# Who makes the lower halves of the first mixer's weights: VectorE instead of GpSimd, with two passes moved to ScalarE

## The chip, the cores and the metric

One core of a Trainium2 chip runs the whole program in one launch. The metric is the device time of one execution in microseconds (us), and the runs shown are compared by their median. A profile of one further execution is read beside them; its times count from the first instruction of the program.

## What is computed

The reference is a two-layer backbone for 256 latent tokens of width 1024, with 256 context tokens as a prefix. Layer 0 mixes tokens with a gated linear recurrence that runs in both directions (RG-LRU), layer 1 with a spatial-gating MLP, and each mixer is followed by a mixture of 64 experts with 8 chosen per token. The change concerns layer 0's mixer alone:

```python
def rglru_mixer(hx, hc, w_in, conv_w, conv_b, r_w, r_b, i_w, i_b, lam, w_out, ctx_out):
    gate_x, ux = jnp.split(hx @ w_in, 2, axis=-1)
    ux = dwconv_centred(ux, conv_w, conv_b)                    # 4 taps along the tokens
    uc = dwconv_centred(hc @ w_in[:, RNN_WIDTH:], conv_w, conv_b)
    for d in range(2):                                         # both directions
        a_c, b_c = lru_coeffs(flip(uc), r_w[d], r_b[d], i_w[d], i_b[d], lam[d], True)
        h_c = linear_scan(a_c, b_c)
        a_x, b_x = lru_coeffs(flip(ux), r_w[d], r_b[d], i_w[d], i_b[d], lam[d], False)
        b_x = b_x.at[:, 0].add(a_x[:, 0] * h_c[:, -1])
        yx = yx + flip(linear_scan(a_x, b_x))
    return (jax.nn.gelu(gate_x) * yx) @ w_out
```

`lru_coeffs` computes, from two 256x256 matrices per head (five heads), r = sigmoid(u r_w + r_b), i = sigmoid(u i_w + i_b), a = exp(8 r logsigmoid(lam)) and b = sqrt(1 - a^2) i u.

## The kernel before

Tokens lie along the free dimension and features along the 128 partitions, 256 latent and 256 context tokens side by side (512 columns). A float32 product is made of three fast ones (`mm3`, L309): both factors are split in an upper part that the fast format holds and a lower part (the rest), and high x high, high x low and low x high are summed, in this order.

**The weight stream.** Every weight tile is 128x2048 (1 MB) and comes in the order of one list, through a ring of eight buffers. For the mixers a tile is cut in four chunks of 128x512. The function `splitter` (L553) makes the two parts of each chunk: ScalarE copies the chunk to `wh` (L563), the engine that `eng(i, c)` names subtracts `wh` from the chunk and writes `wl` (L564). There are four buffers of each. A call `wq(q)` issues all splits up to chunk q+2, at that place of the program.

**The order.** The schedule is written out by hand (`manual_schedule`): each engine runs its instructions in the order in which the Python code issues them. For each head h the order is A(h), C(h), B(h) (L341), with pieces of another matrix product (`ada_step`, the fillers "F") between them; after the five heads come O(0) to O(3) and Q, the product with `w_out`.

- A(h) (L744): 48 matmuls of 512 columns, for two feature tiles i. When the last one of a tile is issued, `wq(q + 3 + 2 * i)` (L769) issues the splits of C's chunks 0, 1 (i=0) or 2, 3 (i=1). Then `conv` (L749): ScalarE applies one tap and the bias (L753), VectorE three taps (L755), a copy to the upper part `us` (L758) and the lower part (L759). At the end `release()` twice (L771) issues `B_end` for the two halves of head h-1.
- C(h) (L852): 48 matmuls of 256 columns and a gelu. Its `wq` calls, and those of the fillers behind it, issue the splits of B's four chunks.
- B(h) (L804): for two halves jt, 24 matmuls of 512 columns into four PSUM banks, that ScalarE takes out with tanh (L817); then a tanh and an exp for each direction (L822, L823), and VectorE's four passes over 128x1024 (L825 to L828). In the second half the calls at L816 and `wq(q + 5)` (L819) issue the splits of the next tile's four chunks, so they stand between the passes of the two halves.
- `B_end` (L831): ScalarE's square root over 128x1024 (L833, it needs another activation table), then on VectorE two memsets, a product (L836), four scans (L840, L843) and a sum (L845). `gated(h)` (L865), issued at the start of the next B, multiplies with the gelu (L868) and splits the product in `zh` and `zl` (L869, L870; on GpSimd for h < 4).
- After A(0) stands `decay()` (L786), a chain of 27 small VectorE instructions that needs a ScalarE exp first.

In the kernel before, `split_eng` (L704) names GpSimd for every tile but the last one (Q), that is for 19 tiles or 76 chunks.

Of the kernel before, what the change touches and what calls it, by code (L numbers as in the profile page):

```python
# [14 lines left out]
AF = mybir.ActivationFunctionType  # L15
OP = mybir.AluOpType
# [285 lines left out]
def _body(nc, tc, a, pp, rp, ps, ps1, dr):  # L302
    V, S, G, PE = nc.vector, nc.scalar, nc.gpsimd, nc.tensor
# [5 lines left out]
    def mm3(out, wh, wl, xh, xl, start, stop):  # L309

        mm(out, wh, xh, start, False)
        mm(out, wh, xl, False, False)
        mm(out, wl, xh, False, stop)

    def bank(shape=(P, 512)):
        return ps.tile(list(shape), F32, name="b")
# [22 lines left out]
    plan0, nf = [], 0  # L339
# [9 lines left out]
    for kind, i in plan0[1:]:  # L349
# [10 lines left out]
        elif kind == "F":  # L360
            l, c, k = fillers[i]
# [68 lines left out]
    onesf = pp.tile([P, P], F32, name="onesf")  # L430
# [23 lines left out]
    def warm(func):  # L454

        S.activation(out=warm_t, in_=onesf[:, 0:1], func=func)
# [96 lines left out]
    def splitter(tmp, tiles, eng, bufs=4):  # L553

        out = []

        def get(q, last=None):
            while len(out) < min(q + 3, last or 4 * len(tiles)):
                i, c = divmod(len(out), 4)
                t = st.tile(tiles[i])[:, 512 * c:512 * c + 512]  # L560
                hi = tmp.tile([P, 512], F32R, name="wh", bufs=bufs)
                lo = tmp.tile([P, 512], F32R, name="wl", bufs=bufs)
                S.copy(out=hi, in_=t)  # L563
                eng(i, c).tensor_tensor(out=lo, in0=t, in1=hi.bitcast(F32), op=OP.subtract)  # L564
                out.append((hi, lo))
                if c == 3:
                    st.free(tiles[i])
            return out[max(q, 0)]

        return get  # L570

    def cut(parts, c):
        return [x[:, c * P:c * P + P] for x in parts]
# [63 lines left out]
    def mixer0(rx):  # L637
      with tc.tile_pool(name="m0", bufs=1) as mp, tc.tile_pool(name="m0t", bufs=2) as tp:
# [3 lines left out]
        def h0(x, k):  # L642
            return h0t[2 * x + k // 4][:, k % 4, :]
# [57 lines left out]
        sx = mp.tile([P, 8], F32, name="sx")  # L701
        sc = mp.tile([P, 8], F32, name="sc")

        def split_eng(i, c):  # L704
            kind, j = plan0[users[i]]
            return G if kind in "ACOB" else V

        users = [i for i, e in enumerate(plan0) if e[0] != "F"]

        base = 8  # L710
        wq = splitter(tp, [2] + [base + i for i in users[1:]], split_eng)

        def first_quarter(b):

# [29 lines left out]
        def A(h, q):  # L744
            uc = tp.tile([P, 2, 2, T], F32, name="uc", bufs=2)
            us = tp.tile([P, 2, 2, 512], F32R, name="us", bufs=1)
            ucs[h] = uc, us

            def conv(i, p):  # L749
                ft = 2 * h + i  # L750
                pv = p.rearrange("p (s t) -> p s t", s=2)
                o = uc[:, i]
                S.activation(out=o, in_=pv, func=AF.Identity, scale=cw[:, 2, ft:ft + 1], bias=cb[:, ft:ft + 1])  # L753
                for kk, (d0, d1, s0_, s1_) in ((0, (2, T, 0, T - 2)), (1, (1, T, 0, T - 1)), (3, (0, T - 1, 1, T))):
                    V.scalar_tensor_tensor(out=o[:, :, d0:d1], in0=pv[:, :, s0_:s1_], scalar=cw[:, kk, ft:ft + 1],  # L755
                                           in1=o[:, :, d0:d1], op0=OP.mult, op1=OP.add)
                of = o.rearrange("p s t -> p (s t)")
                V.tensor_copy(out=us[:, 0, i, :], in_=of)  # L758
                V.tensor_tensor(out=us[:, 1, i, :], in0=of, in1=us[:, 0, i, :].bitcast(F32), op=OP.subtract)  # L759

            ps_ = [bank(), bank()]
            steps = [(i, k) for k in range(8) for i in range(2)] if h == 0 else [(i, k) for i in range(2) for k in range(8)]
            for i, k in steps:
                if h == 0 and i == 0 and k:
                    yield
                wc = divmod(2 * k + i if h == 0 else 8 * i + k, 4)
                mm3(ps_[i], *cut(wq(q + wc[0], 4 if h == 0 and k < 7 else None), wc[1]), h0(0, k), h0(1, k), k == 0, k == 7)
                if k == 7:
                    wq(q + 3 + 2 * i)  # L769
                    conv(i, ps_[i])  # L770
            release()  # L771
            release()
# [31 lines left out]
        def B(h, q):  # L804
            warm(AF.Exp)
            uc, us = ucs.pop(h)
            y = ys[h] = tp.tile([P, 2, T], F32, name="hf", bufs=4)

            for jt in range(2):
                ft = 2 * h + jt  # L810
                ta, te, ti = (tp.tile([P, 2, 512], F32, name=n, bufs=2) for n in ("T", "Tt", "I"))
                for g in range(2):
                    for d in range(2):
                        p = bank()
                        for k in range(2):
                            mm3(p, *cut(wq(q + 2 * jt + g), 2 * d + k), us[:, 0, k, :], us[:, 1, k, :], k == 0, k == 1)  # L816
                        S.activation(out=(ta, ti)[g][:, d, :], in_=p, func=AF.Tanh, scale=0.5, bias=(rb_, ib_)[g][:, d, ft:ft + 1])  # L817
                if jt:
                    wq(q + 5)  # L819
                for d in range(2):  # L820
                    n1, n2 = nz[:, d, ft:ft + 1], nz2[:, d, ft:ft + 1]
                    S.activation(out=te[:, d, :], in_=ta[:, d, :], func=AF.Tanh, scale=n1, bias=n1)  # L822
                    S.activation(out=ta[:, d, :], in_=ta[:, d, :], func=AF.Exp, scale=n2, bias=n2)  # L823
                uv = uc[:, jt].rearrange("p s t -> p (s t)").unsqueeze(1).to_broadcast([P, 2, 512])
                V.scalar_tensor_tensor(out=te, in0=ta, scalar=1.0, in1=te, op0=OP.add, op1=OP.mult)  # L825
                V.tensor_scalar(out=ta, in0=te, scalar1=-1.0, scalar2=1.0, op0=OP.mult, op1=OP.add)
                V.scalar_tensor_tensor(out=te, in0=te, scalar=2.0, in1=te, op0=OP.subtract, op1=OP.mult)
                V.scalar_tensor_tensor(out=ti, in0=ti, scalar=1.0, in1=uv, op0=OP.add, op1=OP.mult)  # L828
                held.append((h, jt, y, ta, te, ti))

        def B_end(h, jt, y, ta, te, ti):  # L831
# [29 lines left out]
        def release():  # L861
            if held:
                B_end(*held.popleft())
# [31 lines left out]
        for i, (kind, j) in enumerate(plan0):  # L895
            if kind == "F":
                l, c, k = fillers[j]
                ada_step(l, c, k, tp)
                wq(4 * sum(u < i for u in users) + 1)
                continue  # L900
            if kind == "O" and j == 0:
                tail = Tail(tp, 0, mod[:, 0, 2, :], rw, "hf", 4)
            if kind == "O" and j == 2:
                warm(AF.Sqrt)
            if kind == "B":
                while done:
                    gated(done.pop())
            if i == 0:
                deque(a0, 0)
                decay()  # L910
                continue
            n = st.reserve({"A": "a_in", "C": "a_in", "B": "gate", "O": "a_out", "Q": "a_out"}[kind])
            deque({"A": A, "B": B, "C": Cg, "O": O, "Q": Q}[kind](j, 4 * users.index(n - base)) or (), 0)
            if kind == "C":
                if j == 1:
                    late_small()
                    S.dma_start(rw, a["r_w"][:, 0])
                if j == 3:
                    V.tensor_copy(out=identb, in_=ident)
                    V.tensor_copy(out=ltrib, in_=C["ltri"])  # L920

                    V.tensor_scalar(out=later["rb"], in0=later["rb"], scalar1=0.5, scalar2=None, op0=OP.add)
                if j == 4:
                    st.grow(rx, "wx", 4)
# [676 lines left out]
    with tc.tile_pool(name="rx", bufs=1) as rx:  # L1601
        tail = mixer0(rx)
        tail = moe(0, tail)
        tail = mixer1(tail)
        moe(1, tail)
# [16 lines left out]
```

## Time and profile before

| | us |
|---|---|
| median of 3 runs | 1510.4 |
| lowest and highest | 1503.66, 1511.35 |
| the profiled execution's own time | 1504.02 |
| its span, first to last instruction | 1502.2 |

Busy shares of the span: TensorE (PE) 94%, VectorE (DVE) 51%, ScalarE (ACT) 35%, GpSimd (POOL) 29%. The mean granted TensorE clock is 0.973 of the full 2.4 GHz. In the rows below, a tile name stands with an arrow from what it is made of (`wl<-wr,wh`); "x" is a count; a bracket at the end of a timeline row is the engine's idle time before the instruction and what ended it. `PEld` is TensorE's weight load, which runs beside the matmuls. The first mixer runs from the start to about 262 us; the rest of the program does not contain any changed line.

### The profile page before, as it was taken

What the parts mean: (1) busy time and instruction counts of PE and PEld (TensorE: products, weight loads), DVE (VectorE), ACT (ScalarE), POOL (GpSimd) and SP (SyncE); (2) the same over time, 40 slices, a digit from 0 to 9 for tenths busy, and PEclk for the clock granted to TensorE, in tenths of its full rate; (3) what the DMA queues carried; (4) which work ended last, traced back from release to release, by engine and by line L of the source; (5) the groups of instructions that cost most, each with busy time, mean ns of one, the idle gap of its engine ahead of it and who ended that gap; (6) DMA issues with size and microseconds to landing.
All of it is one profiled execution on the core that took longest, in us unless ns stands there. A gap on an engine that the chain in (4) does not pass through costs nothing.

```text
span 1502.2 us, 27457 instructions
## 1 busy us (share of the span) xinstructions
PE 1410.3 (94%) x10752; PEld 983.3 (65%) x10752; DVE 766.5 (51%) x1388; ACT 518.9 (35%) x901; POOL 433.7 (29%) x454
## 2 busy tenths in 40 slices
PE   5999898789999999999999999789999999999998
PEld 4767677546567565565747899666656666566665
DVE  6899997623343434334346686532425333333434
ACT  4767673321222222222225544422212212212232
POOL 1666665412222113221101361322212212211210
PEclk9999999899999999999999999899999999999998
DMA  9776575589998999999999854469998999999994
GB/s 376 280 278 228 224 308 224 231 318 377 381 418 358 421 420 406 421 394 420 420 418 380 320 169 153 140 231 391 362 396 358 421 421 409 406 402 422 420 420 168
DMA packets 77446, 514.88 MB, mean 343 GB/s; under 512 B 9856, under 2 KB 10240, under 8 KB 17024
## 3 DMA queue, kind: packets, MB, share of 16 engines
q1 hardware_dynamic: 74720, 508.91, 83.8%
q10 hardware_dynamic: 2592, 4.16, 0.8%
q8 instruction: 86, 1.41, 0.4%
q14 instruction: 48, 0.39, 0.1%
HBM read 511.99 MB, written 1.05 MB: 342 GB/s over the span
## 4 chain that ended last, share of the span: by engine, by line
PE 59%; issue 13%; POOL 3%; DVE 2%; DMA 2%; ACT 1%; ACTq 0%; POOLq 0%; SPq 0%; DVEq 0%
PE b L307 49%; PE s L307 10%; DMA wr<-in_m_gu 2%; POOL S L1399 1%; POOL wl L564 1%; PE b L1475 1%; DMA wr<-in_m_dn 1%; DVE wl L564 1%; DVE h L948 0%; ACT wh L563 0%; PE b L1587 0%; DVE v L1004 0%; DVE xT L1115 0%; DVE v L1067 0%; DVE u L956 0%
## 5 line engine op out<-in xcount | busy, mean ns | idle before, releaser
L564 POOL TENSOR_TENSOR wl<-wr,wh 128x512 fp32r<-128x512 f32 x134 | 208.2, 1570 | 537.0 <-ACT wh L563 534.8
L307 PE MATMUL b<-wr,xg 128*32 128x512 f32 (+2 forms) x1496 | 301.1, 602 | 8.2 <-DMA wr<-in_m_gu 6.3
L563 ACT CAST wh<-wr 128x512 fp32r<-128x512 f32 x256 | 152.4, 618 | 200.8 <-PE b L307 93.6
L307 PE MATMUL b<-wx,xg 128*32 128x512 f32 (+1 forms) x712 | 196.1, 599 | 0.0
L307 PEld LDWEIGHTS b<-wr,xg 128*32 128x32 f32 (+2 forms) x1496 | 83.3, 119 | 130.6 <-issue 107.2
L307 PE MATMUL s<-hh,wh 128*128 128x256 f32 x512 | 153.7, 300 | 6.4 <-ACT wh L563 6.4
L564 POOL TENSOR_TENSOR wl<-wx,wh 128x512 fp32r<-128x512 f32 x48 | 71.4, 1505 | 302.5 <-ACT wh L563 263.5
L1115 DVE SCALAR_TENSOR_TENSOR xT<-b,mod,xT 128x256 f32<-128x256 f32 x304 | 130.0, 478 | 49.1 <-PE b L307 43.2
L564 DVE TENSOR_TENSOR wl<-wr,wh 128x512 fp32r<-128x512 f32 x122 | 100.2, 838 | 104.3 <-ACT wh L563 104.2
L1491 DVE SCALAR_TENSOR_TENSOR Y<-b,gt,Y 128x512 fp32r<-128x512 f32 x88 | 66.1, 751 | 169.4 <-ACT Y L1490 169.4
L307 PE MATMUL s<-hh,wl 128*128 128x256 f32 x512 | 146.9, 287 | 3.4 <-POOL wl L564 3.4
L307 PE MATMUL b<-wr,ht 128*32 128x512 f32 (+2 forms) x752 | 148.1, 599 | 1.5 <-ACT ht L1477 1.4
L307 PE MATMUL s<-hl,wh 128*128 128x256 f32 x512 | 145.9, 285 | 0.0
L1468 DVE TENSOR_TENSOR h<-h,b 128x256 f32<-128x256 f32 x44 | 18.5, 420 | 205.3 <-ACT h L1467 205.3
L307 PEld LDWEIGHTS s<-hh,wh 128*128 128x128 f32 x512 | 99.4, 194 | 36.0 <-issue 28.3
L1490 ACT ACTIVATE Y<-b,gt 128x512 fp32r<-128x512 f32 x88 | 60.5, 687 | 136.0 <-PE b L307 136.0
L1467 ACT ACTIVATE h<-b 128x256 f32<-128x256 f32 x44 | 16.9, 383 | 256.4 <-PE b L307 256.4
L307 PEld LDWEIGHTS s<-hh,wl 128*128 128x128 f32 x512 | 99.4, 194 | 4.5 <-POOL wl L564 4.2
L307 PEld LDWEIGHTS s<-hl,wh 128*128 128x128 f32 x512 | 99.6, 194 | 0.4
L307 PE MATMUL b<-wx,ht 128*32 128x512 f32 (+2 forms) x352 | 99.1, 603 | 0.5 <-ACT ht L1477 0.5
L563 ACT CAST wh<-wx 128x512 fp32r<-128x512 f32 x112 | 66.5, 618 | 93.9 <-PE b L307 48.3
L1399 POOL TENSOR_SCALAR S<-cst,agq 128x32 fp32r<-128x32 f32 (+3 forms) x208 | 82.6, 421 | 49.4 <-PE b L307 49.3
(283 smaller groups left out, 2817.5 us busy)
## 6 DMA issues: line engine op xcount, KB each, us to landing
wr<-in_m_gu SPq DMA_DIRECT2D x173, 1024.0 KB, 11.6
wx<-in_m_gu SPq DMA_DIRECT2D x83, 1024.0 KB, 11.9
wr<-in_m_dn SPq DMA_DIRECT2D x82, 1024.0 KB, 10.8
wx<-in_m_dn SPq DMA_DIRECT2D x40, 1024.0 KB, 9.9
wr<-in_ada_w SPq DMA_DIRECT2D x31, 1024.0 KB, 7.8
wr<-in_a_in SPq DMA_DIRECT2D x10, 1024.0 KB, 8.7
wr<-in_ada SPq DMA_DIRECT2D x8, 1024.0 KB, 12.2
wr<-in_b_v SPq DMA_DIRECT2D x7, 1024.0 KB, 16.3
```

The lines of the kernel that those rows point to most:

```text
L307: PE.matmul(out, lhsT, rhs, start=start, stop=stop, skip_group_check=True)
L563: S.copy(out=hi, in_=t)
L564: eng(i, c).tensor_tensor(out=lo, in0=t, in1=hi.bitcast(F32), op=OP.subtract)
L1115: V.scalar_tensor_tensor(out=xT[:, d, :], in0=y, scalar=mod[:, l, 5, d:d + 1], in1=xT[:, d, :], op0=OP.mult, op1=OP.add)
L1399: (G if b else V).tensor_scalar(out=s[:, tt, i * P + o:i * P + o + wd], in0=C["iota1"][:, j:j + wd], scalar1=agq[:, tt, q:q + 1], scalar2= ...
L1467: S.activation(out=h, in_=p[:, :256], func=AF.Silu)
L1468: V.tensor_tensor(out=h, in0=h, in1=p[:, 256:], op=OP.mult)
L1475: PE.transpose(p[:, k * P:(k + 1) * P], h[:, k * P:(k + 1) * P], ident)
L1490: S.activation(out=hi, in_=p, func=AF.Copy, scale=gts[g])
L1491: V.scalar_tensor_tensor(out=y[:, 1, 512 * c:512 * c + 512], in0=p, scalar=gts[g], in1=hi.bitcast(F32), op0=OP.mult, op1=OP.subtract)
```

## The change

All lower parts of the first mixer's weights are made by VectorE. The copy to `us` and the pass `ta = 1 - te` go from VectorE to ScalarE, and the pass over `ti` is issued ahead of the second pass over `te`.

```diff
-        def split_eng(i, c):
-            kind, j = plan0[users[i]]
-            return G if kind in "ACOB" else V
-
         users = [i for i, e in enumerate(plan0) if e[0] != "F"]
 
         base = 8
-        wq = splitter(tp, [2] + [base + i for i in users[1:]], split_eng)
+        wq = splitter(tp, [2] + [base + i for i in users[1:]], lambda i, c: V)
...
                 of = o.rearrange("p s t -> p (s t)")
-                V.tensor_copy(out=us[:, 0, i, :], in_=of)
+                S.copy(out=us[:, 0, i, :], in_=of)
                 V.tensor_tensor(out=us[:, 1, i, :], in0=of, in1=us[:, 0, i, :].bitcast(F32), op=OP.subtract)
...
                 V.scalar_tensor_tensor(out=te, in0=ta, scalar=1.0, in1=te, op0=OP.add, op1=OP.mult)
-                V.tensor_scalar(out=ta, in0=te, scalar1=-1.0, scalar2=1.0, op0=OP.mult, op1=OP.add)
+                S.activation(out=ta, in_=te, func=AF.Identity, scale=-1.0, bias=onesf[:, 0:1])
+                V.scalar_tensor_tensor(out=ti, in0=ti, scalar=1.0, in1=uv, op0=OP.add, op1=OP.mult)
                 V.scalar_tensor_tensor(out=te, in0=te, scalar=2.0, in1=te, op0=OP.subtract, op1=OP.mult)
-                V.scalar_tensor_tensor(out=ti, in0=ti, scalar=1.0, in1=uv, op0=OP.add, op1=OP.mult)
                 held.append((h, jt, y, ta, te, ti))
```

## Rows read from the trace of the kernel before

**Rows 1.** Window 42 to 262 us: each engine's busy us, granted clock, DMA share, GB/s.

```profile
42.00:262.00 220.00, 204.43 (x1205) 156.61 (x1207) 198.62 (x234) 143.58 (x216) 146.25 (x87) 0.96 0.65 253
```

**Rows 2.** TensorE's largest wait between 40 and 262 us: total us, times, longest.

```profile
PE b L307 <- POOL wl L564: 12.2, 8, 4.7
```

**Rows 3.** TensorE at the start of A(2), from the timeline.

```profile
101.54 0.79 PE L307 MATMUL b<-wx,wl 128*128 128x512 f32 x1 [3.39 <-POOL wl L564]
```

**Rows 4.** Line 564 in the whole trace: ns minimum, median, maximum; first, last start.

```profile
L564 POOL TENSOR_TENSOR wl<-wr,wh x134: 1256/1304/2281, 22.6 to 1454.9; 128x512 fp32r<-128x512 f32 x134
L564 DVE TENSOR_TENSOR wl<-wr,wh x122: 676/692/1777, 280.7 to 1457.9; 128x512 fp32r<-128x512 f32 x122
```

**Rows 5.** VectorE's timeline: end of A(1), B_end, first passes of B(1).

```profile
80.62 2.31 DVE L755 SCALAR_TENSOR_TENSOR uc<-b,cw,uc 128x508 f32<-128x508 f32 x3
82.96 0.44 DVE L758 CAST us<-uc 128x512 fp32r<-128x512 f32 x1
...
90.59 0.06 DVE L834 MEMSET Tt<- 128x1 f32 x1
...
94.85 0.43 DVE L845 TENSOR_TENSOR hf<-hf,Tt 128x256 f32<-128x256 f32 x1
...
95.92 1.22 DVE L825 SCALAR_TENSOR_TENSOR Tt<-T,Tt 128x1024 f32<-128x1024 f32 x1
97.17 0.98 DVE L826 TENSOR_SCALAR T<-Tt 128x1024 f32<-128x1024 f32 x1
...
100.28 2.29 DVE L828 SCALAR_TENSOR_TENSOR I<-I,uc 128x1024 f32<-128x1024 f32 x1
```

**Rows 6.** ScalarE's timeline: end of A(1), then the two halves of B(1).

```profile
75.33 0.77 ACT L753 ACTIVATE uc<-b,cb,cw 128x512 f32<-128x512 f32 x1
76.12 1.28 ACT L833 ACT_TABLE_LOAD   x1
77.41 2.01 ACT L833 ACTIVATE Tt<-Tt 128x1024 f32<-128x1024 f32 x2
79.33 0.60 ACT L563 CAST wh<-wr 128x512 fp32r<-128x512 f32 x1
...
92.57 0.83 ACT L822 ACTIVATE Tt<-T,nz 128x512 f32<-128x512 f32 x1
...
94.99 0.81 ACT L823 ACTIVATE T<-T,nz 128x512 f32<-128x512 f32 x1
95.71 0.60 ACT L563 CAST wh<-wr 128x512 fp32r<-128x512 f32 x1
...
102.47 0.81 ACT L823 ACTIVATE T<-T,nz 128x512 f32<-128x512 f32 x1
```

**Rows 7.** TensorE's timeline: last of A(1), first low of B(1).

```profile
74.55 0.40 PE L307 MATMUL b<-wx,wl 128*128 128x512 f32 x1
...
85.89 0.39 PE L307 MATMUL b<-us,wl 128*128 128x512 f32 x1
```

**Rows 8.** Matmuls on wl of B(0), and of B(4): first and last start.

```profile
L307 PE MATMUL b<-us,wl x16: 388/389/402, 50.2 to 60.9; 128*128 128x512 f32 x16
...
L307 PE MATMUL b<-us,wl x16: 388/389/397, 199.3 to 209.5; 128*128 128x512 f32 x16
```

**Rows 9.** VectorE's timeline: first and last instruction of decay.

```profile
50.85 0.17 DVE L790 TENSOR_SCALAR s<-s 128x20 f32<-128x20 f32 x1
...
58.22 0.18 DVE L802 TENSOR_SCALAR nz<-nz 128x20 f32<-128x20 f32 x1
```

**Rows 10.** Busy time by window, columns as in Rows 1: A(2) behind its stall.

```profile
101.50:107.00 5.50, 5.46 (x13) 4.31 (x14) 4.67 (x4) 2.38 (x4) 5.50 (x3) 0.50 0.01 5
107.20:115.10 7.90, 7.90 (x38) 6.08 (x40) 7.73 (x9) 2.07 (x4) 6.00 (x4) 1.00 0.72 268
```

**Rows 11.** Timelines of ScalarE, then VectorE: the splits of Q, made by VectorE.

```profile
243.06 0.62 ACT L563 CAST wh<-wx 128x512 fp32r<-128x512 f32 x1 [1.02 <-PE b L307]
...
245.79 2.49 DVE L564 TENSOR_TENSOR wl<-wx,wh 128x512 fp32r<-128x512 f32 x4
```

## The prediction

> **What bounds the kernel now.** I read the busy time by window first. In the first mixer TensorE is busy 204.4 of 220 us and VectorE 198.6, while the DMA engines stand at 0.65 [rows 1]: two engines share the limit, and the weight stream isn't it. At most some 16 us of TensorE's idle time could be won here. What the mixer loses is not given back later: the layers behind it read its output. The waits say whose the idle time is: 12.2 us of TensorE's waits end with a lower part made by GpSimd [rows 2], one of them the 3.39 us at the start of A(2) [rows 3]. The timelines say why VectorE is so full. A subtraction of 128x512 takes GpSimd 1304 ns in the median and VectorE 692 [rows 4]; beside GpSimd, VectorE's pass at L828 took 2.29 us, where the pass at L825, of the same kind and shape, took 1.22 [rows 5]. So GpSimd's work is slow itself and stretches VectorE's.
>
> **Which order the change sets.** Every engine works in the order in which the code issues. GpSimd has hardly anything else to do, so now a lower part is made when its `wh` is there. On VectorE it stands in the queue behind the recurrence. The trace has one case: Q's four lower parts, already VectorE's. The last `wh` of them is made by 243.7, and all four subtractions run at 245.79, after the scans and the split of `zh` [rows 11].
>
> In the heads this falls on one place above all. `release()` at the end of A(h) issues both `B_end` of head h-1; the lower parts of B(h)'s chunks are issued after it, in C(h). ScalarE shows this order: square roots at 77.41, the cast for B(1) at 79.33 [rows 6]. GpSimd could run ahead of the scans; VectorE can't. The third matmul of B(h) needs the first of these lower parts. So B(h) will start only after both `B_end`, which now run beside it.
>
> **One head, step by step.** Zero is the end of A(h)'s last matmul (74.95 in head 1 [rows 7]).
>
> 1. ScalarE's tap for the second feature tile: done at +1.2 [rows 6].
> 2. VectorE's three taps 2.31 [rows 5]: +3.5. The copy to `us` moves to ScalarE: the trace shows none there, the nearest row is its cast of the same shape, 0.60 [rows 6]; with two hand-overs I take 0.7: +4.2. The bounds are 0.44, what the copy took on VectorE [rows 5], and 1.3, if a cast is ahead of it.
> 3. The square root's table load (1.28) and first half (1.0) stand behind that copy on ScalarE; now they run at 76.12, before VectorE's taps at 80.62 [rows 5, 6], and are hidden. That cover is gone: +6.5.
> 4. Two `B_end` without GpSimd beside them: 90.59 to 95.28 is 4.7 each [rows 5], so +15.9.
> 5. B(h)'s first lower part, 0.69 [rows 4]: **+16.6**. Now the matmul that needs it starts 10.9 after A's end [rows 7].
> 6. First half of B's matmuls: 7 of 15 steps between first and last of the 16, and the last's 0.4, give 5.2 [rows 8]: +21.8.
> 7. ScalarE's last tanh 0.7, two pairs of tanh and exp 3.2 (92.57 to 95.80 [rows 6]): +25.7.
> 8. L825 takes 1.22; then ScalarE makes `ta` instead of VectorE. Nearest row: its other 128x1024 pass, half of 2.01 for two [rows 6]; bounds are the 0.98 of the removed pass on VectorE [rows 5] and twice 1.0. What is queued behind it on ScalarE is the whole second half of B: +27.9.
> 9. That second half, from its first cast to its last exp: 95.71 to 103.28, 7.6 [rows 6]: +35.5.
> 10. VectorE's three passes that are left: L825 is 1.22. For the other two the trace has only rows beside GpSimd, up to 2.29; I take L825's 1.22 for each, the row without GpSimd ahead of it [rows 5]; the reordering costs nothing, since the pass over `ti` covers ScalarE's `ta`, and would cost 1 without that cover: +39.2.
> 11. Two lower parts for C 1.4, the first `conv` 2.3 + 0.7 + 0.7, two more lower parts 1.4: +45.7. (A(h+1) has run meanwhile, from about +30 to +41.)
> 12. Second `conv`, copy, table load, square root 5.3, two `B_end` 9.4, the lower part 0.7: **+61.1**.
>
> So a period would be 61.1 - 16.6 = 44.5 us. The four periods now take 199.3 - 50.2, or 37.3 each [rows 8]. TensorE reaches B(h+1) some 11 us after A(h+1) and waits for about 9.
>
> On step 10 a rule says otherwise. The Trainium skill (Vector Engine (DVE) Microarchitecture Reference, "7. Points that are easy to get wrong") says that such a pass with two SBUF sources that aren't bf16 runs at half the rate. By it these passes would stay near 2.2, a head would cost 2 us more and the kernel some 10 more than I forecast; L825, with two such sources, took 1.22 [rows 5], so the trace disagrees.
>
> **Before and after the periods.** Head 0 has no `B_end`, but B(0)'s lower parts stand behind `decay()`, which lasts from 50.85 to 58.40 [rows 9]. Four lower parts among the first normalisations delay A(0) by 0 to 2.8; I take 2. ScalarE's copies in the two `conv` add 1, and `decay`'s exp, now behind the second copy, another 1; `decay` itself is 2 shorter without GpSimd beside it. Its end comes at about 60.6, B(0)'s first lower part at 61.3 in place of 50.2: **+11.1** (bounds 6 and 13). In O, one `B_end` and then another with `gated(4)` stand ahead of lower parts; the three chunks in hand cover part of each. I take **+6**, between 0 and both whole, 9.4.
>
> Then the clock. After the 3.39 us stall the granted clock was 0.50 for the next 5.5 us, which passed 13 matmuls, where later 38 took 7.9: 2.8 us lost [rows 10]. That is 1.2 against 2.4 GHz. Five waits of about 9 us should bring such stretches too, partly inside the wait. The periods of before hold part of this already; I add 1.2 per head, **+6**, between 0 and 14.
>
> **The sum.** 11.1 + 4 x 7.2 + 6 + 6 = 52 us, against the profiled execution's 1504.0: 1556. The median of the runs lies 6.4 above that execution, so 1556 to 1562; I write 1558.
>
> **The rivals.**
>
> *VectorE keeps up.* Step 9 carries ScalarE's delays into the next `conv`. If the casts and tanh of the second half come earlier, VectorE reaches each `conv` on time and the period is step 12's +15.9 + 0.7 from A(h+1)'s own end at about +40.8, so 40.8 us. For it: VectorE's stretch beside GpSimd is gone. Against: the queue in step 9 is all ScalarE's. 11 + 4 x 3.5 + 3 + 3 gives 1535.
>
> *The clock stays low.* If each wait brings a whole stretch and another behind the wait for A's lower parts, a head costs 5.6 and not 1.2: 22 more, 1578 to 1585. For it: every long stall of before has such a stretch. Against: a longer wait may hold the stretch inside itself.
>
> *Faster.* The port is all that counts. The lower part of B's first chunk is ready before TensorE needs it, GpSimd's waits (12.2 [rows 2]) and two stretches at half clock (2.8 each [rows 10]) go, and 1504 becomes 1486. The mechanism is L828's row: 2.29 instead of 1.22 [rows 5], ten times over, and the same at the scans. It decides if both `B_end` end within 10.9 us of A's end [rows 7]; step 4 has 15.9 with no delay at all, and this is against it. The Trainium skill (SBUF — State Buffer, "SBUF: two separate sides") has the rule behind it: VectorE, with two SBUF inputs, and GpSimd take one pair of ports in turn, each for a whole instruction; by that rule, the trace agrees, as L828's 2.29 shows.
>
> *Nothing to measure.* What VectorE gains without GpSimd (some 1 us, as at L828, in several instructions of each half head) pays for what it takes over, and the lower parts come as late as GpSimd's do now: 1504 to 1510.
>
> **How the numbers follow.** The forecast has 0.67, VectorE keeps up 0.14, the low clock 0.08, faster 0.06, nothing 0.05. About 0.5% (7.6 us) is what a measurement of this kernel can tell from no change. Slower by more has 0.67 + 0.14 + 0.08 = 0.89. The range holds the forecast with its bounds and the rivals on its side: low, 6 + 4 x 3.5 + 2 over 1504 is 1526, with the median's share 1530; high, 13 + 4 x 8 + 9 + 14 = 68, or 1572, with 6.4 and some of the low clock 1582.
>
> **What would show it.** Right: the timeline has B(h)'s first lower part straight after the sum of the second `B_end`; TensorE's waits in the mixer end mainly with VectorE's `wl`, about 9 us before each B; VectorE's L828 takes about 1.2 and the scans 0.7; a period near 44.5; VectorE's busy time no higher than before, though it does more, since what grows is its idle time. The stretch from 262 on, shifted, is unchanged. Wrong: VectorE's lower parts of B ahead of the scans, TensorE's wait before B below 3 us, or a mixer that ends before 262.

## The result, and the profile after

| | before | after |
|---|---|---|
| median, us | 1510.77 (4 runs) | 1560.51 (4 runs) |
| lowest and highest | 1503.66, 1511.35 | 1553.47, 1561.29 |
| span of the profiled execution | 1502.2 | 1559.5 |

The changed kernel is slower by 3.3%: the ratio is 1.033, with a 95% interval of 1.0287 to 1.0373. By the medians that is 49.7 us; the two profiled executions are 57.3 us apart, because the one of before was short for its kernel (6.7 us under the median) and the one of after was not. In the changed file the line numbers behind L703 are smaller by four, so L825 is now L821, and so on. ScalarE's new pass is L822, VectorE's pass over `ti` L823 (it was L828), the second pass over `te` L824 (L827).

The busy time by window, with the columns of [rows 1], for the mixer (its last matmul now ends at 314.7, and ended at 259.2) and for what follows:

```profile
42.00:315.00 273.00, 213.31 (x1187) 164.15 (x1191) 174.45 (x287) 159.21 (x235) 11.26 (x13) 0.87 0.54 203
315.00:1559.00 1244.00, 1180.83 (x9252) 807.10 (x9244) 539.95 (x1079) 359.19 (x658) 282.34 (x361) 0.98 0.88 356
```

The window is 53 us longer than that of [rows 1], and TensorE has done the same matmuls. VectorE has taken over 76 subtractions (a few of them before 42 us) and given up 20 passes, and its busy time has fallen from 198.6 to 174.5. It works less and comes later. Of the spans' difference of 57.3, 55.5 arise before the mixer's last matmul.

Three of the waits between 40 and 320 us, TensorE's beside [rows 2]:

```profile
DVE Tt L821 <- ACT T L819: 51.9, 10, 9.5
...
PE b L307 <- DVE wl L564: 45.6, 12, 7.8
...
PE b L307 <- ACT wh L563: 14.1, 10, 2.8
```

The place of the largest wait, TensorE at the start of B(1), beside [rows 3, 7]:

```profile
99.67 0.73 PE L307 MATMUL b<-us,wh 128*128 128x512 f32 x2 [0.72 <-ACT wh L563]
108.19 0.80 PE L307 MATMUL b<-us,wl 128*128 128x512 f32 x1 [7.78 <-DVE wl L564]
```

VectorE's timeline up to there, beside [rows 5]:

```profile
92.78 2.31 DVE L751 SCALAR_TENSOR_TENSOR uc<-b,cw,uc 128x508 f32<-128x508 f32 x3
95.83 0.69 DVE L755 TENSOR_TENSOR us<-uc,us 128x512 fp32r<-128x512 f32 x1 [0.74 <-ACT us L754]
98.23 0.06 DVE L830 MEMSET Tt<- 128x1 f32 x1 [1.71 <-ACT Tt L829]
...
107.11 0.42 DVE L841 TENSOR_TENSOR hf<-hf,Tt 128x256 f32<-128x256 f32 x1
107.45 2.49 DVE L564 TENSOR_TENSOR wl<-wr,wh 128x512 fp32r<-128x512 f32 x4
109.86 0.69 DVE L864 TENSOR_TENSOR hf<-hf 128x512 f32<-128x512 f32 x1
120.04 1.23 DVE L821 SCALAR_TENSOR_TENSOR Tt<-T,Tt 128x1024 f32<-128x1024 f32 x1 [9.49 <-ACT T L819]
```

and ScalarE's, beside [rows 6]:

```profile
95.18 0.62 ACT L754 CAST us<-uc 128x512 fp32r<-128x512 f32 x1 [2.53 <-DVE uc L751]
95.82 1.28 ACT L829 ACT_TABLE_LOAD   x1
97.11 1.06 ACT L829 ACTIVATE Tt<-Tt 128x1024 f32<-128x1024 f32 x1
...
101.95 1.13 ACT L563 CAST wh<-wr 128x512 fp32r<-128x512 f32 x2
...
121.30 1.15 ACT L822 ACTIVATE T<-Tt,onesf 128x1024 f32<-128x1024 f32 x1 [1.29 <-DVE Tt L821]
```

Read the two side by side. The copy to `us` waits 2.53 us on ScalarE for VectorE's taps; behind it stand the table load and the square root, and VectorE idles 0.74 and 1.71 us for them. Both `B_end` run from 98.23 to 107.53. B(1)'s four lower parts follow in one piece, though the last of their upper parts was made at 103.08, and TensorE goes on at 108.19, as soon as the first (107.45 and 0.69) is there. Then VectorE idles 9.49 us, because B has only now begun.

The low matmuls of B(0) and of B(4), beside [rows 8]:

```profile
L307 PE MATMUL b<-us,wl x16: 388/389/797, 62.2 to 74.4; 128*128 128x512 f32 x16
...
L307 PE MATMUL b<-us,wl x16: 387/389/793, 248.5 to 261.4; 128*128 128x512 f32 x16
```

The period is (248.5 - 62.2) / 4 = 46.6 us, where it was 37.3.

### The profile page after: what moved, and what is told of

The parts are those of the page before. It is cut to its first block, busy times and chain, and to the rows that moved or that the text cites. A ratio compares the mean times of both kernels' runs of the same rounds, so it can differ in the third digit from the quotient of the medians.

```text
span 1559.5 us, 27434 instructions
## 1 busy us (share of the span) xinstructions
PE 1419.0 (91%) x10752; PEld 990.3 (64%) x10752; DVE 743.0 (48%) x1444; ACT 535.9 (34%) x921; POOL 293.8 (19%) x378
## 4 chain that ended last, share of the span: by engine, by line
PE 57%; issue 12%; DMA 3%; DVE 3%; POOL 2%; ACT 1%; ACTq 0%; SPq 0%; POOLq 0%; DVEq 0%
PE b L307 47%; PE s L307 9%; DMA wr<-in_m_gu 2%; POOL S L1395 1%; POOL wl L564 1%; PE b L1471 1%; DMA wr<-in_m_dn 1%; DMA wx<-in_m_gu 1%; DVE wl L564 1%; DVE h L944 0%; DVE v L1063 0%; ACT wh L563 0%; DVE v L1000 0%; DVE xT L1111 0%; DVE u L952 0%
## 5 line engine op out<-in xcount | busy, mean ns | idle before, releaser
L564 DVE TENSOR_TENSOR wl<-wr,wh 128x512 fp32r<-128x512 f32 x186 | 142.1, 787 | 117.0 <-ACT wh L563 116.9
L564 POOL TENSOR_TENSOR wl<-wr,wh 128x512 fp32r<-128x512 f32 x70 | 94.3, 1357 | 476.2 <-ACT wh L563 474.6
L564 POOL TENSOR_TENSOR wl<-wx,wh 128x512 fp32r<-128x512 f32 x36 | 49.9, 1398 | 301.8 <-ACT wh L563 262.8
L307 PE MATMUL b<-S,xt 128*128 128x256 f32 x704 | 94.1, 287 | 0.0
## 6 DMA issues: line engine op xcount, KB each, us to landing
wx<-in_m_gu SPq DMA_DIRECT2D x83, 1024.0 KB, 12.1
```

The source lines that it names most:

```text
L307: PE.matmul(out, lhsT, rhs, start=start, stop=stop, skip_group_check=True)
```

## The experiments

The theory, *queue order*: the loss comes from where the lower parts stand in VectorE's queue, and from hand-overs that the ScalarE passes put into the same chain. The rival, *VectorE's load*: the time follows the amount of work on VectorE. In the table, "first low" is the start of the first matmul of B(0) that reads a lower part of a weight, and the period is a quarter of the time from there to the same matmul of B(4), both from TensorE's timeline of each run. Each ratio is to runs of the kernel before that were made along with that run: one group is e1 to e4, one e5 to e8, one e9 to e11. The medians of before, in these groups and with the result, lie between 1505.1 and 1510.8, so across groups the ratios and the traces say more than the medians. Behind Q's last matmul nothing differs between the kernels, and yet the thirteen traces take from 1242.0 to 1251.1 us there; a few microseconds of a total can come from that alone.

| run | median us | ratio to before (95%) | first low | period |
|---|---|---|---|---|
| before | 1505 to 1511 | 1 | 50.2 | 37.3 |
| after | 1560.5 | 1.033 (1.0287 to 1.0373) | 62.2 | 46.6 |
| e1, lower parts alone | 1540.2 | 1.0194 (1.0168 to 1.022) | 59.8 | 42.7 |
| e2, ScalarE passes alone | 1519.4 | 1.0069 (1.0051 to 1.0088) | 54.6 | 39.4 |
| e3, B's lower parts by GpSimd | 1522.3 | 1.0085 (1.0066 to 1.0104) | 57.7 | 39.3 |
| e4, releases moved into B | 1531.0 | 1.0141 (1.012 to 1.0163) | 61.6 | 40.0 |
| e7, B's and O's by GpSimd | 1523.5 | 1.0101 (1.0072 to 1.0131) | 57.9 | 39.4 |
| e8, A's and C's by VectorE | 1512.7 | 1.004 (1.0021 to 1.0058) | 53.2 | 38.1 |
| e10, copy back on VectorE | 1550.0 | 1.0296 (1.0272 to 1.032) | 60.0 | 44.3 |
| e11, all on VectorE, order mended | 1523.3 | 1.0124 (1.0099 to 1.0149) | 55.1 | 40.3 |
| e5, gate product late | 1499.8 | 0.9953 (0.9937 to 0.9969) | 50.8 | 35.9 |
| e6, e5 and C's by VectorE | 1503.0 | 0.9965 (0.9952 to 0.9979) | 51.1 | 37.0 |
| e9, e5, last one early | 1500.7 | 0.9958 (0.9938 to 0.9979) | 50.2 | 36.2 |

### Order or load: e4 and e3

e4 changes no instruction and no engine:

```diff
         # A, at its end
-            release()
-            release()
...
             if kind == "B":
+                release()
+                release()
                 while done:
                     gated(done.pop())
```

> The changed kernel with every instruction on the same engine; only the two releases (which issue both B_end of the head before) move from the end of A to the start of B, so that on VectorE they stand behind B's lower parts. Queue order: the wait of 7.8 us ahead of each B goes, a new one of 2 to 4 us comes at the start of the next A (its lower parts stand behind the first half's passes, which now stand behind B_end): period 38 to 39.5, B(0) still behind decay, about 1524 us. VectorE's load: not one instruction more or less on any engine, so 1560 us.

Measured: 1531.0 us and a period of 40.0. Some 30 of the 50 us come back without moving any work from one engine to another, so these 30 are not load. The time is 7 us above the forecast of 1524, since the new wait was forecast too small: at the start of A(2), A(3) and A(4) the upper parts come late as well. TensorE's two largest waits between 40 and 300 us in e4:

```profile
PE b L307 <- DVE wl L564: 18.6, 8, 4.9
PE b L307 <- ACT wh L563: 17.0, 6, 3.9
```

ScalarE makes those upper parts behind its new pass, and that pass waits for VectorE's first pass of the half; both now run after `B_end`.

e3 leaves the releases and gives 20 chunks back to GpSimd:

```diff
-        ... lambda i, c: V)
+        ... lambda i, c: G if plan0[users[i]][0] == "B" else V)
```

> The changed kernel, with only the lower parts of the five B tiles (20 of 76 chunks) back on GpSimd, whose queue has no scans. Queue order: B no longer waits for B_end, the period falls to 36 or 37 us and the half-clock stretches with the waits go; B(0) no longer waits for decay either. About 1500 to 1512 us, that is nearly the whole loss of 50 back for a quarter of the chunks. VectorE's load: a quarter of the chunks gives a quarter of the loss back, about 1547 us.

Measured: 1522.3. A quarter of the chunks returns three quarters of the loss, far from the rival's 1547. It misses the forecast's 1500 to 1512 by 10 us. Most of the miss has two places. One is the period, 39.3 and not 36 to 37; at the start of A(2) two waits are left:

```profile
110.08 0.74 PE L307 MATMUL b<-wx,wh 128*128 128x512 f32 x2 [1.66 <-ACT wh L563]
112.77 0.80 PE L307 MATMUL b<-wx,wl 128*128 128x512 f32 x1 [1.95 <-DVE wl L564]
```

The second wait is for the lower part behind the passes of B's first half, which I had counted. The first is again for ScalarE's upper part, which I had not. The other place is B(0): its first low comes at 57.7, 7.5 us later than in the kernel before, although its lower parts no longer stand behind `decay`. ScalarE's timeline shows why:

```profile
53.52 0.62 ACT L754 CAST us<-uc 128x512 fp32r<-128x512 f32 x1 [2.53 <-DVE uc L751]
54.05 0.21 ACT L784 ACTIVATE s<-lam 128x20 f32<-128x20 f32 x1
54.28 1.28 ACT L785 ACT_TABLE_LOAD   x1
55.57 0.22 ACT L785 ACTIVATE s<-s 128x20 f32<-128x20 f32 x1
55.70 1.12 ACT L563 CAST wh<-wr 128x512 fp32r<-128x512 f32 x2
```

The last line makes B(0)'s upper parts. They stand behind `decay`'s exp and its table load, and these behind the copy to `us`, which waits 2.53 us for VectorE's taps. By e2 (the ScalarE passes alone, 54.6) and e8 (lower parts of A and C alone, 53.2), 4.4 of the 7.5 go with the passes and 3.0 with A(0)'s lower parts.

### The two halves of the change: e1, e10 and e2

e1 is the kernel before with `lambda i, c: V` alone; e10 the changed kernel with one line back:

```diff
-                S.copy(out=us[:, 0, i, :], in_=of)
+                V.tensor_copy(out=us[:, 0, i, :], in_=of)
```

> All lower parts by VectorE as in the change, but the copy to us and the pass ta = 1 - te stay on VectorE, in the old order. Theory 'queue order' (B of a head waits for both B_end, which stand ahead of its lower parts on VectorE, and each ScalarE pass in the changed kernel is one more hand-over on that chain): most of the loss stays, but a head's period falls by about 4 us against the changed kernel's 46.6 (square root hidden again 1.8, two copies 0.5, ScalarE not held by VectorE's first pass 2.3, less 0.6 for the pass back on VectorE), so about 1541 us. Rival 'VectorE's load' (the time follows how much work VectorE has): VectorE gets 20 more instructions than in the changed kernel, so 1560 or more.

> The changed kernel with the copy to us back on VectorE; the pass ta = 1 - te stays on ScalarE. This separates the two hand-overs that the run with the lower parts alone took away together (period 46.6 to 42.7). Queue order: the square root's table load no longer stands behind a copy that waits for VectorE: 1.8 us, and two copies 0.5 us, so a period of 44.3 us, 4 x 2.3 less in all, and B(0) some 1 us earlier: 1549 to 1552 us. Rival 'the pass on ScalarE is what costs' (ScalarE held by VectorE's first pass): period stays at 46 or more, 1557 to 1561 us.

Measured: e1 1540.2 and a period of 42.7 where 46.6 less 4 was forecast; e10 1550.0 and 44.3, as forecast. (The period is the better witness for e10: its group's median of before is 1505.1, the intervals of its ratio and the changed kernel's overlap, and by its ratio of 1.0296 e10 would have some 1555 beside a before of 1510.8.) So of the changed kernel's 9.3 us per head above the one before, taken away one after the other, the copy is 2.3, the pass over `ta` and the reordering together 1.6, and the lower parts' place 5.4, net of what VectorE gains without GpSimd beside it. The copy, and the pass with the reordering, made VectorE's work less and the period longer. e10's ScalarE timeline shows what the copy had uncovered: with it gone, the table load follows ScalarE's tap at once, while VectorE is still at its convolutions.

```profile
86.97 0.77 ACT L749 ACTIVATE uc<-b,cb,cw 128x512 f32<-128x512 f32 x1
87.76 1.28 ACT L829 ACT_TABLE_LOAD   x1
89.06 2.01 ACT L829 ACTIVATE Tt<-Tt 128x1024 f32<-128x1024 f32 x2
```

e2 is the changed kernel with `"ACOB"` on GpSimd again:

> The two passes on ScalarE and the reordering alone; lower parts by GpSimd as in the kernel before. Queue order: the new hand-overs cost about as much as VectorE saves, since ScalarE now stands behind VectorE and the square root's table load is no longer hidden: 1505 to 1520 us. VectorE's load: 20 passes fewer on a VectorE that is 95% busy, some 20 us of work, so faster than before, about 1495 us.

Measured: 1519.4, the upper end of the forecast and slower than before by 0.7%, where the rival had 1495. Relieving VectorE, which is 95% busy from 86 to 245 us of the trace of before, did not pay, because the relief added waits between it and ScalarE. TensorE's waits from 40 us to O's end in e2 show it; the second line has no counterpart in the kernel before:

```profile
PE b L307 <- POOL wl L564: 12.0, 8, 2.5
PE b L307 <- ACT wh L563: 11.6, 6, 3.4
```

### The O stage: e7, and the rest on VectorE: e8

Both are edits of the same line: `"BO"` on GpSimd in the changed kernel, and `"OB"` in the kernel before.

> The changed kernel with the lower parts of the five B tiles and of the four O tiles (36 of 76 chunks) on GpSimd. Against the run with B alone on GpSimd (1522.3) this tests the O stage by itself: there TensorE waits 4.7 and 2.6 us for lower parts that stand behind a B_end on VectorE, and 3.7 for the upper part before the first of them. Queue order: those of VectorE go, the clock drop behind them too: 1511 to 1515 us. VectorE's load: 16 of 76 chunks more, a fifth of the loss of 50: 1512 us as well, so this run sizes the term of O and doesn't tell the two apart; what does is where the time goes: by queue order all of it behind 240 us of the trace.

> The kernel before with the lower parts of A and C on VectorE (40 of 76 chunks), those of B and O on GpSimd; no pass on ScalarE. Queue order: B and O lose their waits for B_end; what stays is a wait of about 1.8 us at the start of each A, whose lower parts stand behind the passes of B's first half, where the kernel before has waits of 1 to 5 us: about the kernel before, 1503 to 1513 us. VectorE's load: half of the chunks on VectorE and ten copies and ten passes more than in the changed kernel: above 1530 us.

e7 measured 1523.5, not 1511 to 1515, and can't be told from e3 by the ratios either (1.0101 and 1.0085). In the traces the stage from O(0) to the mixer's end is 43.9 us long and was 47.7 in e3: there the term is some 4 us, but the times of the runs don't show it. In O(1) TensorE's waits of e3 (4.74 us for VectorE's lower part, and 3.71 for an upper part) became these:

```profile
241.10 0.38 PE L307 MATMUL b<-zh,wh 128*128 128x256 f32 x1 [3.37 <-ACT wh L563]
243.52 0.58 PE L307 MATMUL b<-zh,wl 128*128 128x256 f32 x1 [1.92 <-POOL wl L564]
```

e8 measured 1512.7, inside its forecast and far from the rival's 1530: 40 chunks on VectorE cost 0.4%. The theory's reason, that none of them stands right behind a `B_end`, fits the trace, in which TensorE's waits for VectorE's lower parts are the four at the start of an A; they are 11.7 us together, more than the 1.8 each that was forecast.

### All on VectorE, in another order: e11

e1 with e4's releases, and `decay()` called at the start of B(0):

> All lower parts on VectorE, no pass on ScalarE, and the order mended: both B_end of the head before, and decay, are issued at the start of B, behind B's lower parts. VectorE does more here than in any other run. Queue order: B(0)'s first lower part at about 54 us, no wait ahead of B, 2 to 4 us of waits at the start of A: period 38 to 39, the O stage 4 us longer than before: 1512 to 1522 us. VectorE's load: the slowest of all, above 1540 us, like the run with the lower parts alone.

Measured: 1523.3, against e1's 1540.2 with the same instructions on the same engines, and 1 us above the forecast. The waits before B are gone from B(1) on; the one at the next A is 5 us and not 2 to 4:

```profile
110.95 0.80 PE L307 MATMUL b<-wx,wl 128*128 128x512 f32 x1 [5.04 <-DVE wl L564]
```

So order alone gives back 17 us by the medians; by the ratios (1.0194 and 1.0124) it is some 10 and by the end of Q's last matmul in the two traces (290.5 and 277.0) 13.5. It doesn't give back all: with `B_end` behind B's lower parts, the next A's stand behind `B_end`.

### Better than both: e5, e6 and e9

The kernel before had the same fault on GpSimd, smaller: its lower parts for A(h+1) stood behind the split of the gate product, which waits for a VectorE instruction behind the scans; the 3.39 us of [rows 3] are such a wait. GpSimd's timeline in the kernel before:

```profile
96.07 1.54 POOL L869 CAST zh<-hf 128x512 fp32r<-128x512 f32 x1 [6.43 <-DVE hf L868]
97.69 1.59 POOL L870 TENSOR_TENSOR zl<-hf,zh 128x512 fp32r<-128x512 f32 x1
99.24 6.70 POOL L564 TENSOR_TENSOR wl<-wr,wh 128x512 fp32r<-128x512 f32 x3
```

e5 moves that step:

```diff
                 held.append((h, jt, y, ta, te, ti))
+            while done:
+                gated(done.pop())
...
-            if kind == "B":
-                while done:
-                    gated(done.pop())
```

> The kernel before with one step moved: the product with the gelu and its split (VectorE L868, GpSimd L869 and L870) are issued at the end of B instead of its start, so that on GpSimd the next A's lower parts no longer stand behind an instruction that waits for VectorE's scans. Queue order: the waits at the start of A (0.99, 3.39, 0.87, 4.75 us) and the two half-clock stretches (2.6 us each) go; VectorE, 95% busy, gives part of it back: 1500 to 1506 us against 1510. VectorE's load: no instruction changes its engine, so 1510 us.

> As the run with the late gate product, and C's lower parts on VectorE, where they stand between the passes of B and the convolutions, ahead of when C needs them. Queue order: no new wait on TensorE; four subtractions more per head on VectorE (2.7 us), four of GpSimd's less beside it (some 3 to 4 us of stretch less): the same as that run or up to 4 us faster, 1497 to 1506 us. VectorE's load: 20 subtractions more, a quarter of the loss: 1522 us.

> The kernel with the late gate product, but the one of head 3 again at the start of B(4): in that run TensorE waits 5.2 us at 218 us, in O(0), for head 3's zh, which GpSimd makes late. Queue order: this wait goes and nothing comes in its place, since O(0)'s lower parts had no wait behind the early zh in the kernel before: 1493 to 1497 us where that run had 1499.8.

e5 measured 1499.8, ratio 0.9953, just under the forecast's 1500: faster than both kernels by one moved step. The gain over the kernel before is half a per cent; the interval leaves out 1, and in the traces Q's last matmul ends 5.0 us earlier (251.1 for 256.1). The waits at the start of A did not all go: behind B(0) and up to O, TensorE's waits for GpSimd's lower parts fell from 10.0 to 6.8 us. e6 (C's chunks on VectorE as well) fell in its forecast at 1503.0, no faster than e5; in its trace Q's last matmul ends at 255.7, so there none of e5's 5.0 us shows. e9 puts head 3's product back to the start of B(4) and should have saved the 5.2 us that TensorE waits for it in O(0):

```profile
217.85 0.58 PE L307 MATMUL b<-zh,wh 128*128 128x256 f32 x1 [5.19 <-POOL zh L871]
```

The wait is gone, and the time is 1500.7 (ratio 0.9958), the same and not the 1493 to 1497 of the forecast. In e9's O stage these came instead, four of 0.54 (the kernel before has four such as well) and then one ahead of Q:

```profile
218.37 0.39 PE L307 MATMUL b<-zh,wl 128*128 128x256 f32 x1 [0.54 <-POOL wl L564]
...
241.27 0.46 PE L307 MATMUL b<-zh,wh 128*128 128x256 f32 x1 [2.21 <-DVE zh L871]
```

TensorE came to Q earlier and waited there for head 4's `zh`, behind VectorE's last `B_end`. That wait of 2.21 is the old one (2.2 in the kernel before); e5 did not have it. VectorE made head 4's `zh` at 240.98 in e5 and at 240.70 in e9:

```profile
240.98 0.43 DVE L871 CAST zh<-hf 128x512 fp32r<-128x512 f32 x1
```

So VectorE's chain set when Q could start, and in e5 a wait in front had been covering one behind.

## Why the prediction was right

The forecast was 1558 and the median 1560.5; the mechanism and the place hold, and the size holds in part by luck. Between the two profiled executions, from which the terms were read, the sum was to be 52 us and was 57.3; the medians lie 49.7 apart, where 1558 meant 47.6. By its steps:

- **The order.** Right: the four lower parts of B follow the second `B_end` without a gap, e4 and e11 move the time by moving the order alone, and e3 by putting B's lower parts in a queue without scans.
- **One head.** 44.5 without the clock was forecast. In the trace the period is 46.6, and the 46 matmuls behind the wait of B(1) took 13.4 us where 10.6 is usual, 2.8 more. The period without the clock is then about 43.8.
- **Step 1.** Too early for head 1, where it had VectorE ready for its taps at +1.2. A(1)'s last matmul ended at 88.5 and the taps began at 92.78, at +4.3; the first low, forecast at +16.6, came at +19.7:

```profile
88.12 0.40 PE L307 MATMUL b<-wx,wl 128*128 128x512 f32 x1
```

  VectorE was as late in the first head as steps 9 to 11 make it in the next. Those steps put the next head's first low some 20 after its A's end (61.1 less 41), and heads 2 to 4 measure 19.7 to 20.5. The period is the lap from one to the next, so it did not suffer.
- **Steps 2 and 3.** The copy took 0.62 and VectorE idled 0.74 for it (0.7 forecast). From the copy's end (95.80) to the first `B_end` (98.23) it was 2.43 where 2.3 was forecast, 1.71 of it idle time of VectorE. e10 weighs both together at 2.3 per head, as was forecast for that run.
- **Steps 4 and 5.** 9.3 for two `B_end` (9.4), the first lower part 0.69.
- **Steps 8 to 10.** ScalarE's pass took 1.15 (1.0). The two passes that no row had shown without GpSimd took 1.22 each, the value taken:

```profile
L823 DVE SCALAR_TENSOR_TENSOR I<-I,uc x10: 1217/1218/1222, 74.3 to 271.3; 128x1024 f32<-128x1024 f32 x10
...
L824 DVE SCALAR_TENSOR_TENSOR Tt<-Tt x10: 1224/1226/1226, 75.6 to 272.6; 128x1024 f32<-128x1024 f32 x10
```

  The rule of half rate for such passes, which the Trainium skill has (Vector Engine (DVE) Microarchitecture Reference, "7. Points that are easy to get wrong"), does not give the 2.2 us that the prediction worked out by it: VectorE's plain product of two such tiles (L832) takes 1.22 as well. The measurement decides; with bf16 sources no run shows these passes.
- **B(0).** 62.2 for 61.3: +12.0 where +11.1 was forecast. A(0) ended 3.3 later (46.4 for 43.1) and not 2; `decay` lasted 5.5 for 7.6, 2 shorter as forecast. e11's 55.1 for e1's 59.8 shows 4.7 that belong to `decay`'s place.
- **The clock.** Mis-sized: 1.2 us per head and 6 in all were taken, on the ground that the periods of before hold part of it already. But the 44.5 of the sum was built from steps at full clock, so the whole stretch had to be added. B(1)'s window behind the wait shows it, with the columns of [rows 10]:

```profile
104.00:114.00 10.00, 5.81 (x14) 4.61 (x15) 6.40 (x11) 1.96 (x4) 1.90 (x2) 0.50 0.82 300
114.00:121.00 7.00, 7.00 (x33) 5.78 (x32) 0.96 (x1) 4.42 (x6) 0.00 (x0) 1.00 0.42 162
```

  TensorE had stood idle from 100.4 to 108.2; it went on at the lower level, 1.2 GHz, to 114.0. A longer wait did not hold the stretch inside itself. Of the five B, the 46 matmuls behind the wait lost 1.7 to 2.9 each against 10.6, together 12.1.
- **The O stage.** Mis-sized the other way: from O(0) to the mixer's end it took 47.6 us, before 44.0: +3.6, where +6 was taken with the clock apart.

The terms now: B(0) 12.0, four periods 4 x 9.3 = 37.3, B(4) up to O(0) 2.7, O 3.6, behind the mixer 1.7; together 57.3, the spans' difference. The last of them is within what the unchanged part varies by. The errors in clock and O were of opposite sign, and part of the agreement is owed to that; part is owed to the base, since the sum was set on an execution that lay over 6 us under its kernel's median. Of the rivals, *VectorE keeps up* fell, since ScalarE's second half of B took 7.6 us as forecast and ran behind the new pass, and the first lows of heads 1 to 4 came 19.7 to 20.5 after A's end, not 16.6. *The clock stays low* fell: it had 5.6 us for each head, and the five B lost 12 together. *Nothing to measure* fell with the 3.3%. *Faster* described something real: in e1, which takes nothing off VectorE and gives it all the subtractions, VectorE's busy time from 42 us to the mixer's end is 185.2 us and was 196.9. But both `B_end` ahead of B(1) ended only 19.0 us after A(1)'s end in the changed kernel, where that rival needed 10.9, and e1 shows that the change without a ScalarE pass leaves the kernel 1.9% slower.

## What to carry to other kernels

Before a step moves to another engine, read which instructions stand ahead of it in that engine's queue and who waits for it: a faster engine that reaches it later is the slower one. A pass moved to relieve a full engine can add a hand-over in each direction, and hold up whatever the other engine was running ahead with, here a table load and the next casts. In this kernel, with two engines both near full, moving the order (e5, one step) was worth more than moving the work.

## What was not expected

That VectorE's busy time would not rise was forecast, but not that it would fall by 24 us in the mixer, while VectorE took over the subtractions (0.69 us each) and gave up 20 passes. e1, which gives up none, still has 12 us less. GpSimd beside it had been stretching many of its instructions by about 1 us: L828 took 2.30 in the mean and takes 1.22, the scans took 1.13 and take 0.72. And a wait can be free: e5 waits 5.2 us for a tile, e9 doesn't, and both take the same time.
